# A two-layer decoder trunk on one core: operand offsets of the weight pieces, tried in the up projections

## The chip, the cores and the metric

The kernel runs on one core of a Trainium2 chip. The metric is the device time of one execution in microseconds (us); the time of a kernel is the median of its runs.

## The reference

The program computes two decoder layers on 256 tokens of width 2048, in float32, and a final RMSNorm. Each layer projects the normalised input once, runs three token mixers side by side (retention, dilated attention, a gated positional mixing), sends their 2048 channels through an output projection, and then a gated feed-forward with a short causal convolution. Cut to what matters here:

```python
proj = rms_norm(x, norm1_w) @ w_in                       # 2048 -> 6400
mixed = concat(retention(...), dilated_attention(...), chunk_gmlp(...))
x = x + mixed @ w_out                                    # 2048 -> 2048
h = rms_norm(x, norm2_w) @ w_up                          # 2048 -> 2 x 5632
gate, val = split(causal_conv3(h))                       # width 3, per channel
x = x + (silu(gate) * val) @ w_down                      # 5632 -> 2048
```

Nearly all the arithmetic is in the four weight matrices of each layer.

## The kernel before, in words

All weights lie in DRAM as one stream in the order in which they are used, 792 pieces of 128 x 1024 float32, 396 per layer. SyncE's queue loads a piece into a raw buffer (line 115). ScalarE writes a rounded copy of it, `hi` (line 140), and VectorE the rest, `lo` = raw - `hi` (line 150). The activations are split in the same way. A product is then three matmuls, hi x hi, hi x lo and lo x hi, so that a piece is always 24 matmuls of 128 x 128 by 256 columns. `Weights.take` (line 156) hands out the pieces and has them split three pieces ahead of their use; the order of all work is written out by hand, with generators that run small pieces of the mixers between the pieces of weights.

There are two kinds of stage. In the feature-major ones (`proj_t`, line 371, its matmul on line 388) a 128-column block of the piece is the stationary operand and the activations stream past it. These are the q and k projections (pieces 0 to 23 and 36 to 59 of a layer), the output projection (100 to 131) and the feed-forward (132 to 395). In the token-major ones (`proj_n`, line 417, matmul on line 428) the activations are stationary and the piece streams: pieces 24 to 35 (the v projection of the attention) and 60 to 99. `token_major` (line 81) tells which is which. The feed-forward has three parts of 96, 96 and 72 pieces; in each the first 64, 64 and 48 are the up projection and the others the down projection.

The mixers' own small float32 matmuls and transposes (lines 235 and 239, helpers) run between pieces: from piece 36 to the first pieces of the output projection, and for each norm. They set a flag, `stirred`.

`hi` and `lo` are tiles of 1024 + 64 columns in four buffers each, and the piece lies in its tile at an offset, in elements, that `place` (line 104) chooses when the split is issued:

```python
PLACES = ((32, 0), (0, 32))
...
    def place(self, p):
        other = self.stirred and p - self.moved >= APART
        if other:
            self.stirred, self.moved = False, p
        a = PLACES[token_major(p)][other]
        return slice(a, a + PIECE)
```

So a feature-major piece lies at 32 and a token-major one at 0; the first piece placed after small matmuls, at least four behind the last such, lies at the other of the two. It is called a moved piece below. In layer 0 these are 10, 14, 39, 43, 47, 51, 55, 59, 63, 75, 79, 83, 87, 91, 95, 99, 103, 107, 137 and 141; layer 1 has them at 401, 405 and then in the same places from 435 on, up to 537.

Of the kernel before, what the change touches and what calls it, by code (L numbers as in the profile page):

```python
# [27 lines left out]
P = 128  # L28
D = 2048
# [13 lines left out]
PIECE = 1024  # L43
# [7 lines left out]

SLACK = 64
PLACES = ((32, 0), (0, 32))
LAYER_PIECES = TOTAL // PIECE // DEPTH
QK_PIECES = 2 * H * D // PIECE
AV_PIECES = H * D // PIECE
REST_PIECES = (2 * H + 2 * G) * D // PIECE
APART = 4
FFN_PARTS = ((0, 16), (16, 32), (32, 44))


# [19 lines left out]
def token_major(p):  # L81

    p %= LAYER_PIECES
    a, b = QK_PIECES + AV_PIECES, 2 * QK_PIECES + AV_PIECES
    return QK_PIECES <= p < a or b <= p < b + REST_PIECES


class Weights:
# [13 lines left out]
        self.moved = 0  # L102

    def place(self, p):
        other = self.stirred and p - self.moved >= APART
        if other:
            self.stirred, self.moved = False, p
        a = PLACES[token_major(p)][other]
        return slice(a, a + PIECE)

    def load(self, upto):
# [69 lines left out]
def trunk_kernel(tc, x0, xt, stream, par, cst, wst, lnw, out):  # L181
# [5 lines left out]
    with ctx:  # L187
# [454 lines left out]
        for l in range(DEPTH):  # L642
# [124 lines left out]

            for i, (f0, f1) in enumerate(FFN_PARTS):
                last = i == len(FFN_PARTS) - 1
                QX[:] = [None] * NK  # L770
# [105 lines left out]
```

## Time and profile before

| | |
|---|---|
| median of 2 runs | 2243.12 us (2242.28 to 2243.97) |
| the profiled execution | 2242.37 us, span 2240.6 us |
| TensorE busy | 2223.4 us, 99% of the span |
| VectorE, ScalarE busy | 64%, 51% |
| granted TensorE clock, mean | 0.998 |
| DMA queue of the weights | 55.2% of 16 engines' span |

The busy time of TensorE adds up overlapping matmuls; how fast they follow each other is read from the length of a stretch over the number of matmuls in it. The chain of work that ended last lists such stretches, in order of time, by line.

### The profile page before, as it was taken

How to read it: one execution, taken by the hardware profiler on the slowest of the kernel's cores; microseconds unless marked ns; L12 is line 12 of the kernel's file. 1: busy time of each engine (PE TensorE's matmuls, PEld its weight loads, DVE VectorE, ACT ScalarE, POOL GpSimd, SP SyncE). 2: the span in 40 equal slices, each digit the busy share in tenths (PEclk: the TensorE clock that was granted, in tenths of full speed). 3: DMA queues.
4: the chain of work that ended last, by engine and by line, in shares of the span. 5: the costliest groups of instructions: out<-in, count | busy, mean ns of one | idle time of the engine just before them, and what ended most of it. 6: DMA issues, size and time to landing. Idle time of an engine off the chain costs nothing.

```text
span 2240.6 us, 45994 instructions
## 1 busy us (share of the span) xinstructions
PE 2223.4 (99%) x19430; PEld 2220.2 (99%) x19430; DVE 1443.3 (64%) x2086; ACT 1143.9 (51%) x1616; POOL 24.4 (1%) x38
## 2 busy tenths in 40 slices
PE   8999999999999999999999999999999999999997
PEld 8999999999999999999999999999999999999997
DVE  6466556677657775577754655666775577756775
ACT  6465455555435554455544745555554355434554
POOL 0000100000000000000000001000000000000000
PEclk9999999999999999999999999999999999999999
DMA  8545456565555555565565454555555565555553
GB/s 293 189 152 195 158 173 199 189 195 194 193 198 190 196 188 199 183 205 190 196 203 174 169 179 170 179 191 196 191 195 196 183 205 192 195 194 193 197 190 123
DMA packets 117135, 425.15 MB, mean 190 GB/s; under 512 B 12992, under 2 KB 12992, under 8 KB 116800
## 3 DMA queue, kind: packets, MB, share of 16 engines
q1 hardware_dynamic: 116928, 422.21, 55.2%
q8 instruction: 152, 2.49, 0.5%
q14 instruction: 55, 0.45, 0.1%
HBM read 420.06 MB, written 2.10 MB: 188 GB/s over the span
## 4 chain that ended last, share of the span: by engine, by line
PE 99%; DMA 0%; DVE 0%; SPq 0%; ACT 0%; POOLq 0%; issue 0%; DVEq 0%
PE mm L388 84%; PE mm L428 13%; PE mx L235 2%; PE mx L239 0%; DMA xg<-in_xt_dram 0%; DVE xg L786 0%; SPq L125 0%; SPq L261 0%; POOLq L870 0%; DVEq L870 0%; ACT p L290 0%; DVE diag L350 0%; DVE xg L718 0%; ACT t L312 0%; DVE ms L346 0%
## 5 line engine op out<-in xcount | busy, mean ns | idle before, releaser
L150 DVE TENSOR_TENSOR lo<-raw,hi 128x1024 fp32r<-128x1024 f32 (+1 forms) x793 | 969.3, 1223 | 694.1 <-ACT hi L140 693.6
L140 ACT ACTIVATE hi<-raw 128x1024 fp32r<-128x1024 f32 (+1 forms) x793 | 837.4, 1058 | 851.3 <-PE mm L388 459.5
L388 PE MATMUL mm<-p,hi 128*128 128x256 f32 x7168 | 1234.9, 277 | 5.7 <-ACT hi L140 5.1
L388 PEld LDWEIGHTS mm<-p,hi 128*128 128x128 f32 x7168 | 1085.1, 188 | 6.9 <-ACT hi L140 5.1
L388 PE MATMUL mm<-p,lo 128*128 128x256 f32 x3584 | 991.6, 277 | 0.0
L388 PEld LDWEIGHTS mm<-p,lo 128*128 128x128 f32 x3584 | 674.4, 188 | 0.5 <-DVE lo L150 0.2
L388 PE MATMUL mm<-q,hi 128*128 128x256 f32 x3840 | 655.2, 276 | 0.0
L388 PEld LDWEIGHTS mm<-q,hi 128*128 128x128 f32 x3840 | 578.6, 188 | 0.0
L388 PE MATMUL mm<-q,lo 128*128 128x256 f32 x1920 | 530.1, 276 | 0.0
L388 PEld LDWEIGHTS mm<-q,lo 128*128 128x128 f32 x1920 | 360.5, 188 | 0.0
L428 PE MATMUL mm<-hi,p 128*128 128x256 f32 x1664 | 273.8, 280 | 0.0
L428 PEld LDWEIGHTS mm<-hi,p 128*128 128x128 f32 x1664 | 232.3, 189 | 0.0
L428 PE MATMUL mm<-lo,p 128*128 128x256 f32 x832 | 180.2, 279 | 0.0
L750 ACT ACTIVATE a<-hs,prm 128x256 f32<-128x256 f32 x176 | 104.3, 593 | 63.3 <-DVE hs L402 63.3
L428 PEld LDWEIGHTS mm<-lo,p 128*128 128x128 f32 x832 | 133.8, 188 | 0.0
L753 DVE SCALAR_TENSOR_TENSOR a<-hs,prm,a 128x256 f32<-128x256 f32 x176 | 85.4, 485 | 6.3
L752 DVE SCALAR_TENSOR_TENSOR a<-hs,prm,a 128x256 f32<-128x256 f32 x176 | 84.2, 478 | 4.4 <-ACT a L750 4.4
L718 DVE TENSOR_TENSOR xg<-xg,mm 128x256 f32<-128x256 f32 x128 | 53.4, 419 | 39.3 <-PE mm L388 39.3
L402 DVE TENSOR_TENSOR hs<-mm,rbc 128x256 f32<-128x256 f32 x176 | 73.6, 418 | 2.7 <-PE mm L388 2.7
L756 ACT ACTIVATE a<-a 128x256 f32<-128x256 f32 x88 | 35.7, 405 | 33.5 <-DVE a L753 33.5
L312 ACT ACTIVATE t<-xg 128x256 f32<-128x256 f32 x75 | 30.1, 408 | 42.2 <-DVE xg L718 41.3
L762 ACT ACTIVATE q<-a 128x256 fp32r<-128x256 f32 x88 | 35.5, 404 | 3.5 <-DVE a L759 3.5
(107 smaller groups left out, 562.0 us busy)
## 6 DMA issues: line engine op xcount, KB each, us to landing
raw<-in_stream_dram SPq DMA_DIRECT2D x791, 512.0 KB, 3.8
out_dram<-xg SPq DMA_DIRECT2D x8, 256.0 KB, 2.4
xg<-in_xt_dram SPq DMA_DIRECT2D x3, 512.0 KB, 8.7
cs<-in_cst_dram SPq DMA_DIRECT2D x1, 1216.0 KB, 8.5
raw<-in_stream_dram SPq DMA_DIRECT2D x2, 256.0 KB, 4.1
ws<-in_wst_dram SPq DMA_DIRECT2D x2, 256.0 KB, 5.2
lw<-in_lnw_dram SPq DMA_DIRECT2D x2, 256.0 KB, 5.4
prm<-in_par_dram SPq DMA_DIRECT2D x1, 412.0 KB, 6.1
```

The lines of the kernel that those rows point to most:

```text
L140: self.nc.scalar.activation(hi[:, h], src[:, h], AF.Copy)
L150: self.nc.vector.tensor_tensor(lo[:, h], src[:, h], hi[:, h].bitcast(F32), op=ALU.subtract)
L235: T.matmul(*args, **kw)
L388: T.matmul(acc[m], w, v, start=k == 0 and i == 0, stop=k == n - 1 and i == 2)
L402: V.tensor_tensor(out, acc, norm["bc"], op=ALU.mult)
L428: T.matmul(acc[j][:, c], v, w[:, c], start=k == 0 and i == 0 and c.start == 0, stop=k == NK - 1 and i == 2, skip_group_check=True)
L718: V.tensor_tensor(X[m], X[m], acc, op=ALU.add)
L750: A.activation(a, hs[:, 2 : S + 2], AF.Identity, scale=conv_col(ch, 2), bias=conv_col(ch, 3))
L752: V.scalar_tensor_tensor(a, hs[:, 1 : S + 1], conv_col(ch, 1), a, op0=ALU.mult, op1=ALU.add)
L753: V.scalar_tensor_tensor(a, hs[:, 0:S], conv_col(ch, 0), a, op0=ALU.mult, op1=ALU.add)
L756: A.activation(a, a, AF.Silu)
L762: A.activation(q[:, 0:S], a, AF.Copy)
```

## The change

Two things change in `place`, and nothing else in the program. First, in the up projections the pieces go in groups of eight, and every other group lies at an offset from a list, 11 groups in each layer; between them the pieces lie as before. The list has 22 entries with 18 different values. Second, no token-major piece is moved any more, and the piece ahead of a token-major stage (23 and 59 of a layer) always is. By the flag's course through the program, the moved pieces of layer 0 are then 10, 14, 23, 39, 43, 47, 51, 55, 59, 100, 104, 108, 137 (141 falls into a tried group), and of layer 1 401, 405, 419, 435 and so on in the same places.

```diff
+TRIED = ((31, 33, 28, 36, 30, 34, 24, 40, 8, 56, 16), (48, 12, 20, 44, 52, 60, 4, 28, 33, 36, 56))
...
+FFN_AT = 2 * QK_PIECES + AV_PIECES + REST_PIECES + D * D // P // PIECE
...
     def place(self, p):
-        other = self.stirred and p - self.moved >= APART
+        last = token_major(p + 1)
+        other = not token_major(p) and (last or self.stirred and p - self.moved >= APART)
         if other:
             self.stirred, self.moved = False, p
         a = PLACES[token_major(p)][other]
+        q = p % LAYER_PIECES - FFN_AT
+        if q >= 0:
+            part, r = divmod(q, 96)
+            if r < (64, 64, 48)[part] and r // 8 % 2:
+                a = TRIED[p // LAYER_PIECES][part * 4 + r // 16]
         return slice(a, a + PIECE)
```

The tried groups of layer 0 are pieces 140 to 147, 156 to 163, 172 to 179, 188 to 195, then from 236 and from 332 on in the same rhythm, the last being 364 to 371; in layer 1 they are 396 later.

## Rows read from the trace of the kernel before

**Rows 1.** The page: busy time of the engines (share, instructions), granted clock in 40 slices.

```profile
PE 2223.4 (99%) x19430; PEld 2220.2 (99%) x19430; DVE 1443.3 (64%) x2086; ACT 1143.9 (51%) x1616; POOL 24.4 (1%) x38
...
PEclk9999999999999999999999999999999999999999
```

**Rows 2.** Waits of TensorE's matmuls: who for whom, us, times, longest.

```profile
PE mm L388 <- ACT hi L140: 5.1, 1, 5.1
```

**Rows 3.** The chain in order of time: start, length (us), engine, line, matmuls.

```profile
36.58 40.82 PE mm L388 x360
77.40 33.92 PE mm L428 x288
...
180.32 8.18 PE mm L388 x72
188.50 33.08 PE mm L428 x288
...
408.87 715.38 PE mm L388 x6312
...
1185.55 33.92 PE mm L428 x288
...
1517.02 709.96 PE mm L388 x6264
```

**Rows 4.** Timeline of TensorE around piece 63: start, length, line, operation, operands, count.

```profile
198.00 0.63 PE L428 MATMUL mm<-hi,p 128*128 128x256 f32 x4
...
198.71 0.63 PE L428 MATMUL mm<-hi,p 128*128 128x256 f32 x4
...
200.11 0.62 PE L428 MATMUL mm<-hi,p 128*128 128x256 f32 x4
...
200.79 0.62 PE L428 MATMUL mm<-hi,p 128*128 128x256 f32 x4
```

**Rows 5.** The same around piece 75, which runs from 233.78 to 236.61.

```profile
232.88 0.62 PE L428 MATMUL mm<-hi,p 128*128 128x256 f32 x4
...
233.56 0.62 PE L428 MATMUL mm<-hi,p 128*128 128x256 f32 x4
...
234.25 0.63 PE L428 MATMUL mm<-hi,p 128*128 128x256 f32 x4
...
234.96 0.63 PE L428 MATMUL mm<-hi,p 128*128 128x256 f32 x4
...
237.07 0.62 PE L428 MATMUL mm<-hi,p 128*128 128x256 f32 x4
...
237.75 0.50 PE L428 MATMUL mm<-hi,p 128*128 128x256 f32 x3
```

**Rows 6.** The chain from 218 to 330 us: token-major stretches between small matmuls.

```profile
231.21 13.73 PE mm L428 x120
...
246.90 5.56 PE mm L428 x48
...
253.80 14.14 PE mm L428 x120
...
268.60 8.29 PE mm L428 x72
...
281.50 14.14 PE mm L428 x120
```

**Rows 7.** The chain from 170 to 200 us: six transposes between two pieces.

```profile
179.67 0.65 PE mx L239 x6
```

**Rows 8.** The page's groups: the splits, and two VectorE operations of the convolution.

```profile
L150 DVE TENSOR_TENSOR lo<-raw,hi 128x1024 fp32r<-128x1024 f32 (+1 forms) x793 | 969.3, 1223 | 694.1 <-ACT hi L140 693.6
L140 ACT ACTIVATE hi<-raw 128x1024 fp32r<-128x1024 f32 (+1 forms) x793 | 837.4, 1058 | 851.3 <-PE mm L388 459.5
...
L753 DVE SCALAR_TENSOR_TENSOR a<-hs,prm,a 128x256 f32<-128x256 f32 x176 | 85.4, 485 | 6.3
L752 DVE SCALAR_TENSOR_TENSOR a<-hs,prm,a 128x256 f32<-128x256 f32 x176 | 84.2, 478 | 4.4 <-ACT a L750 4.4
```

## The prediction

> **What bounds the kernel now.** I read the page first, then the waits, then the chain, then single stretches of the timeline. The page shows TensorE busy 99% of the span, its clock granted in full in every slice [rows 1], that is the 2.4 GHz level. The waits show that it waits for its operands in one place only, 5.1 us at the start [rows 2]. So the time is the sum of the matmuls, and the only question is the pace at which they follow each other. The chain gives it, as length divided by count. In the feed-forward of layer 0 it is 715.38 us / 6312 = 113.3 ns, in that of layer 1 709.96 / 6264 = 113.3 ns; in the first token-major stage it is 33.92 / 288 = 117.8 ns, in both layers [rows 3]. Same shapes, same clock, two paces: I call them short (113.3) and long (117.8). A piece is 24 matmuls, so a piece at the long pace costs 24 x 4.45 = 107 ns more.
>
> What switches between them? The stretch of 288 matmuls that starts at 188.50 takes 33.08 us [rows 3]: 4 pieces long and 8 short (96 x 117.8 + 192 x 113.3 = 33.07). Its timeline shows where: six matmuls take 0.71 us up to 198.71 and 0.68 us after 200.11 [rows 4]. The fourth piece (63) is a moved one; the pace is long before and in it, short behind it. Around piece 75 it goes the other way: 0.68 us for six before it, 0.71 in it, 0.68 once it is over [rows 5]. So the pace depends on where the operands lie, it holds once taken, and a moved piece can reset it. It does not always: the stretches of 120 at 253.80 and 281.50 hold a moved piece each (83 and 91) and run at 117.8 throughout [rows 6]. By the tiles' addresses in the program, the stationary operand's start minus the moving one's is 64 modulo 256 bytes in an ordinary piece and 192 in a moved one, in both kinds of stage.
>
> **Tried offsets.** An offset a gives 64 + 4(a - 32) bytes. 22 groups of 8 pieces get one, 18 different values in all: 176 pieces, 4224 matmuls, all in stretches that run at 113.3 now. No instruction, transfer or wait is added. The trace shows one distance beside the ordinary one, 192, and it gives both answers: the 15 pieces at 36.58 hold two moved ones (10 and 14) and keep 113.4, each feed-forward stretch holds two (137, 141; 533, 537) and keeps 113.3 [rows 3], but piece 75 loses the short pace at once [rows 5]. For the 18 values I bound the cost from above by the long pace, the only other one in long stretches: 4224 x 4.45 = +18.8 us; and from below by the quickest pace of any matmul that loads as many weight columns, the transposes at 0.65 / 6 = 108.3 ns [rows 7]: 4224 x -5.0 = -21 us. The nearest rows are the two paces themselves, and they divide evenly, so I take half of the pieces at the long one: 88 x 0.107 = **+9.4 us**.
>
> Here a rule speaks for no effect at all. The Trainium skill, "TensorE: Matmul & The Clock Gate", Step-by-step: what each phase is for, has two independent read ports of the memory for the two operands, so that loading the next weights takes nothing from the running matmul. By that rule the tried offsets would cost 0; the trace disagrees so far, since the pace changes at piece 75, where the offset is all that changes.
>
> **Coming back.** Each group ends with a step back to the ordinary distance, 22 steps. Without small matmuls between, a moved piece at the long pace was followed by the short pace in three places that rows show (63, 75, 87 [rows 3, 5, 6], 87 by 8.29 us for 72, one long piece), against 83 and 91 where it stayed long; at 75 and 87 the pace before was short, at 83 and 91 long. So a return from a group entered at the short pace mostly restores it. I take two of some eleven long groups to stay long through the 8 pieces behind: 16 x 0.107 = **+1.7 us**; ends 0 and the whole feed-forward (below).
>
> **Token-major stages.** They are 52 pieces per layer. Piece by piece 36 of them are long now, 16 short: 12 of 12 and 4 of 12 in the stretches at 77.40 and 188.50 [rows 3], and by length over count of those behind 1 of 5, 1 of 2, 5 of 5, 1 of 3 and 5 of 5 [rows 6]; of eight more, which small matmuls cut up (72, 73, 89, 95 to 99), 7. A moved piece now stands ahead of each stage (23 and 59; 59 was one already), and the eight within (63, 75, 79, ..., 99) go. Piece 59 tells what the first does: it ran at the short pace (8.18 us for 72 with 57 and 58), and the stage behind it began at the long one all the same (4 long pieces) [rows 3]. So I expect 24 to 35 to stay long, and 60 to 71 to run long throughout, now that 63 resets nothing: the 33.08 us become 33.92, +8 pieces per layer. Against that 75, 87 and 99 are no longer moved and may stay short. Later pieces follow the small matmuls between, whose outcome I leave as it is. Net some +6 pieces per layer: 12 x 0.107 = **+1.3 us**. Ends: all of both stages short, -72 pieces, -7.7 us; all long, +32 pieces, +3.4 us. Behind the stage the moved pieces are 100, 104 and 108 where they were 103 and 107: at most a few pieces either way, **+0.3 us**.
>
> **Splits into odd offsets.** ScalarE and VectorE write and read the pieces at the new offsets. VectorE's reads of a row one element off (line 752) take 478 ns, from its start (line 753) 485 [rows 8]: nothing. If it were not nothing, a split of 1.06 + 1.22 us stands three pieces (8.2 us) ahead, and the two engines are busy 51% and 64% of the span [rows 1]. Without that lead the pair's 2.28 us would still fit a piece's 2.72. I cost it at 0. TensorE's own reads from offsets 31, 33, 30 and 34, five groups, 40 pieces, no row shows. The Trainium skill, "SBUF — State Buffer", Door 1: The DMA port swizzle, speaks of 16-byte lines with a penalty for each access that crosses to a new one; such a start would touch one line more, and the page has no price for it. I leave these groups in the half above.
>
> **Sum.** 9.4 + 1.7 + 1.3 + 0.3 = +12.7 us on the profiled execution's 2242.4 us, whose span is 2240.6; it lies 0.7 us under the median of 2243.1. That gives 2255 to 2256; I write **2255**.
>
> **Rivals.**
> - *The distance doesn't matter once the short pace is held.* (It is also what the rule of the two ports would give.) For it: the moved pieces of the feature-major stages at 36.58 and in the feed-forward lost nothing [rows 3], and all tried pieces are of that kind. Against it: piece 75. Then only the token-major and later terms are left: 2243 + 1.6 = 2245. Chance 0.22.
> - *The long pace sticks.* The first tried group (piece 140) takes it, and the step back restores nothing, as at 83 and 91 [rows 6]; nothing else in the feed-forward resets it, since no small matmuls run there. Pieces 140 to 395 and 536 to 791 would be long: 512 x 0.107 = 55 us, 2298, **slower** than before. It decides from 420 long pieces on (2%, 45 us). Against it: the returns at 63, 75 and 87. The full case 0.05; in part, or some distance with a pace above 117.8 that no row shows, between 2268 and 2288, another 0.11.
> - *A tried distance is better than the ordinary one,* or the moved piece ahead sets a whole stage to the short pace. 113.3 is not the floor of the engine [rows 7]. If a quarter of the groups went to 108.3, 44 pieces x 24 x 5 ns = 5 us would come back; with the stages short 7.7 more: 2243 - 13 = 2230. Against it: 792 pieces show two paces and neither is under 113.3. Chance 0.10.
> - *The forecast,* a third to two thirds of the tried pieces long: +6 to +12 us for them, 2247 to 2264 with the other terms. Chance 0.52.
>
> **Numbers.** The range 2237 to 2278 takes in the forecast, the first rival, the near half of the third and the near part of the second; some 0.15 is outside. 2% of this kernel is 45 us, about what a measurement can tell from no change. Over that on the fast side only all groups at 108.3 with both stages short and more would come (21 + 7.7 = 29 us): 0.01. On the slow side the sticking case with a little for a worse pace: 0.06. Within: 0.93.
>
> **What would show it.** In the chain after, length over count of the two feed-forward stretches: 113.3 ns throughout means that distance doesn't matter, 113.3 + 4.45/3 = 114.8 that all tried pieces (a third of them) are long. Group by group, 192 matmuls in 21.8 us or in 22.6. The stage at 188.50 at 33.08 or 33.92 us tells whether 63 did the reset; the one at 77.40 at 32.6 us would show that the moved piece ahead works, which I don't expect. A pace over 118 or under 113 in any group would prove my bounds wrong; an ordinary group at the long pace, that returns don't restore.

## The result and the profile after

The changed kernel takes 2272.65 us (2 runs, 2272.57 and 2272.73) against 2243.12: ratio 1.0135, 95% interval 1.0119 to 1.0152. That is 29.5 us slower, under 2%, inside the range of 2237 to 2278, and more than twice the 12 us that were forecast. The profiled execution took 2272.57 us, its span is 2270.8, 30.2 longer than before.

The page after: span and instructions, then busy time of the engines.

```profile
span 2270.8 us, 45994 instructions
...
PE 2253.6 (99%) x19430; PEld 2250.8 (99%) x19430; DVE 1443.2 (64%) x2086; ACT 1144.0 (50%) x1616; POOL 24.7 (1%) x38
```

The waits after: the longest of TensorE's.

```profile
PE mm L397 <- ACT hi L149: 5.1, 1, 5.1
```

TensorE's busy time grew by 30.2 us, as much as the span; VectorE's and ScalarE's are the same to 0.1 us, at the same counts [rows 1]. So no split became dearer. TensorE's waits are as before, the longest 5.1 us at the start [rows 2]: the matmuls follow each other more slowly. The chain of the kernel after (start, length, line, matmuls; line 397 is 388 of before, 437 is 428) has the places:

```profile
77.87 33.92 PE mm L437 x288
...
188.97 33.92 PE mm L437 x288
...
409.55 731.30 PE mm L397 x6312
...
1202.44 33.92 PE mm L437 x288
...
1313.54 33.92 PE mm L437 x288
...
1534.13 723.58 PE mm L397 x6264
```

Against [rows 3] the two feed-forward stretches grew by 15.9 and 13.6 us, 29.5 together; the stage at 77.87 is unchanged, and the one at 188.97 lost the short pace of its last eight pieces, 0.84 us. The same view cut to single groups in the feed-forward of layer 0, and to two of layer 1 (a cut shows one matmul more than the group's 192):

```profile
422.94 23.06 PE mm L397 x193
...
445.89 21.89 PE mm L397 x193
...
467.66 22.84 PE mm L397 x193
...
490.38 22.73 PE mm L397 x193
...
823.28 23.15 PE mm L397 x193
...
1067.12 67.96 PE mm L397 x577
...
1547.52 22.89 PE mm L397 x193
...
1903.65 22.52 PE mm L397 x193
```

Length over count: the group at offset 31 runs at 119.5 ns, the ordinary one behind it at 113.4; the group at 33 at 118.3, and the ordinary one behind it stays at 117.8; the group at 40 at 119.9 (120.0 by the starts of its matmuls). Behind the layer's last tried group (offset 16) all 24 pieces that are left run at 117.8. The last two rows are the groups at 48 and 4 of layer 1, at 118.6 and 116.7, the latter, with the group at 8, the quickest of all. The starts of the matmuls in the trace give each group's mean pace:

| distance, modulo 256 (offset) | ns a matmul | distance (offset) | ns a matmul |
|---|---|---|---|
| 64 (32), ordinary | 113.3 or 117.8 | 112 (44) | 120.0 |
| 192 (0), moved | 113.3 or 117.8 | 128 (48) | 118.6 |
| 0 (16) | 120.0 | 144 (52) | 119.9 |
| 16 (20) | 118.3 | 160 (56), twice | 120.0, 120.0 |
| 32 (24) | 118.3 | 176 (60) | 118.1 |
| 48 (28), twice | 118.3, 117.8 | 208 (4) | 116.7 |
| 56 (30) | 117.8 | 224 (8) | 116.7 |
| 60 (31) | 119.5 | 240 (12) | 117.3 |
| 68 (33), twice | 118.3, 118.3 | 80 (36), twice | 118.8, 118.8 |
| 72 (34) | 118.3 | 96 (40) | 120.0 |

No tried distance runs at the short pace. The table holds for these groups as they were entered here; in other kernels below, 208 and 240 run at another pace. Piece by piece against the trace of before the 30.2 us are: tried groups 22.4; pieces behind them that stay long 7.5 (69 pieces: 8 each behind 33, 28, 20, 60 and again 33, and behind 16 the 24 left and 5 of the next layer's first); token-major stages 0.6; output projection -0.2; the opening, pieces 0 to 23, 0.5; the end of the program -0.5 (rounded).

### The profile page after: what moved, and what is told of

The parts are those of the page before. It is cut to its first block, busy times and chain, and to the rows that moved or that the text cites. A ratio compares the mean times of both kernels' runs of the same rounds, so it can differ in the third digit from the quotient of the medians.

```text
span 2270.8 us, 45994 instructions
## 1 busy us (share of the span) xinstructions
PE 2253.6 (99%) x19430; PEld 2250.8 (99%) x19430; DVE 1443.2 (64%) x2086; ACT 1144.0 (50%) x1616; POOL 24.7 (1%) x38
## 4 chain that ended last, share of the span: by engine, by line
PE 99%; DMA 0%; DVE 0%; SPq 0%; ACT 0%; POOLq 0%; issue 0%; DVEq 0%
PE mm L397 84%; PE mm L437 13%; PE mx L244 2%; PE mx L248 0%; DMA xg<-in_xt_dram 0%; DVE xg L795 0%; SPq L134 0%; SPq L270 0%; POOLq L879 0%; DVEq L879 0%; ACT p L299 0%; DVE diag L359 0%; DVE xg L727 0%; ACT t L321 0%; DVE ms L355 0%
## 5 line engine op out<-in xcount | busy, mean ns | idle before, releaser
L397 PE MATMUL mm<-p,hi 128*128 128x256 f32 x7168 | 1262.6, 280 | 5.7 <-ACT hi L149 5.1
L397 PEld LDWEIGHTS mm<-p,hi 128*128 128x128 f32 x7168 | 1096.1, 189 | 6.8 <-ACT hi L149 5.1
L321 ACT ACTIVATE t<-xg 128x256 f32<-128x256 f32 x75 | 30.2, 409 | 41.5 <-DVE xg L727 40.6
```

The lines of the kernel that those rows point to most:

```text
L397: T.matmul(acc[m], w, v, start=k == 0 and i == 0, stop=k == n - 1 and i == 2)
```

## The experiments

The theory after the result: a matmul stream can hold 113.3 ns only where the stationary operand's start minus the moving one's is 64 or 192 bytes modulo 256; any other distance tried costs 3 to 7 ns a matmul; and at 64 or 192 the stream may still be stuck at 117.8, depending on how it was entered. Its rivals: the weights' own alignment counts, not the distance; the jump counts, not the distance; the new stage rule has a part in it. All kernels of this section but the two with a ratio were run once. The kernel before alone ranges from 2241.59 to 2244.65 us over its runs here, so totals 1 or 2 us apart say nothing by themselves; the readings rest on the lengths of stretches, such as the 715.38 us of the first feed-forward, which come back to the last digit wherever no piece changes its pace.

**The stage rule alone.** The changed kernel without the list.

```diff
-            if r < (64, 64, 48)[part] and r // 8 % 2:
+            if False and r < (64, 64, 48)[part] and r // 8 % 2:
```

> The rule for the token-major stages alone (a moved piece ahead of each, none within), no tried offsets. By the ledger of the changed kernel the two stages together gained 0.6 us and the output projection lost 0.2, so this should take 2243 to 2244 us, with the token-major pieces at the same paces as in the changed kernel: 24 to 35 and 60 to 71 long (117.8 ns a matmul), 95 to 99 short (113.3). If part of the 22 us of the tried groups came from the changed stages ahead of them, the feed-forward would show pieces at the long pace here too; I expect none.

Measured 2241.87 us, beside 2241.64 for the kernel before on the same chip. The chain:

```profile
77.10 33.92 PE mm L437 x288
...
188.20 33.92 PE mm L437 x288
...
408.79 715.38 PE mm L397 x6312
```

Both stages are long throughout, as in the changed kernel, and the feed-forward is as in [rows 3]. The rule has no part in the 29.5 us of the feed-forward; the 0.2 us between the two totals can't be told from nothing.

**The tried offsets alone.** The changed kernel with `place`'s first lines of before.

```diff
-        last = token_major(p + 1)
-        other = not token_major(p) and (last or self.stirred and p - self.moved >= APART)
+        other = self.stirred and p - self.moved >= APART
```

> The tried offsets alone, with the stage rule of before. By the ledger of the changed kernel the tried groups cost 22.4 us, the ordinary pieces behind them 4.4 in the up projections and 2.0 in the down projections, and some 0.5 at the second layer's start, which the first layer's last group leaves long. That is 29.3 us: 2271 to 2272 us. If the two parts of the change influence each other, the feed-forward would show other returns than in the changed kernel; I expect the same six.

Measured 2271.89 us. The chain:

```profile
188.27 33.08 PE mm L436 x288
...
408.64 731.30 PE mm L396 x6312
...
1533.01 723.58 PE mm L396 x6264
```

The feed-forward is that of the changed kernel to the last digit, with the same six returns stuck. The two parts add up and don't touch each other.

**Both operands 64 bytes further.** The kernel before with a longer tile in front of everything.

```diff
-        warm = cp.tile([P, 2], F32, name="warm")
+        warm = cp.tile([P, 18], F32, name="warm")[:, 16:18]
```

> The kernel before, with 64 bytes put in front of all the tiles that matmuls read, so that weights and activations both move by 64 bytes and the distance between them stays (64 modulo 256, 192 in moved pieces). Theory: only the distance counts; then 2242 to 2244 us and 113.3 ns in the feed-forward. Rival: the weights have to start at a multiple of 128 bytes, whatever the activations do; then every piece is at a longer pace, 792 x 24 x some 5 ns = +95 us, 2335 to 2340.

Measured 2241.91 us, beside 2241.64. The chain:

```profile
77.35 33.92 PE mm L428 x288
...
188.45 33.08 PE mm L428 x288
...
408.82 715.38 PE mm L388 x6312
```

Lengths equal to [rows 3] to the last digit, with all weights off the multiples of 128 bytes. So at this shift it doesn't matter where the operands lie, only how far apart. Other shifts of both were not run.

**Another distance everywhere, without jumps.**

```diff
-PLACES = ((32, 0), (0, 32))
+PLACES = ((48, 16), (16, 48))
```

> The kernel before with all offsets 16 elements higher: feature-major pieces at 48, moved ones at 16, token-major ones at 16 and 48. The distance is then 128 or 0 modulo 256 in every piece, and there are no jumps in the feed-forward but the two moved pieces. Theory (the short pace exists only at 64 modulo 128): all of the feed-forward runs at 118.5 to 120 ns, and the kernel takes 19008 x about 5.3 ns = 100 us less what is long already (10 us), 2325 to 2340 us. Rival (it is the jump from one distance to another that throws the matmuls into the long pace, and any distance holds the short one when left alone): 113.3 ns in the feed-forward, 2240 to 2250 us.

Measured 2336.09 us, 94 more than before, with the same instructions. The chain:

```profile
79.79 34.55 PE mm L428 x288
...
194.20 34.53 PE mm L428 x288
...
422.04 749.07 PE mm L388 x6312
...
1577.40 743.39 PE mm L388 x6264
```

749.07 / 6312 = 118.7 ns, the pace of the group at 48 in the table, now held through 263 pieces without a tried jump; the token-major stages, at distance 0, run at 120.0, as the group at 16 does. The distance is enough by itself.

**The same jumps to distance 192.** The tried groups at 0 and 64, which both give 192, with the stage rule of before.

```diff
-TRIED = ((31, 33, 28, 36, 30, 34, 24, 40, 8, 56, 16), (48, 12, 20, 44, 52, 60, 4, 28, 33, 36, 56))
+TRIED = ((0, 64) * 6, (64, 0) * 6)
...
-        last = token_major(p + 1)
-        other = not token_major(p) and (last or self.stirred and p - self.moved >= APART)
+        other = self.stirred and p - self.moved >= APART
```

> The tried groups at offsets 0 and 64 in place of the 18 values, stage rule as before: as many jumps, but the distance is 192 modulo 256 in each group, 64 modulo 128. Theory: the short pace is kept in all 22 groups and behind them, 113.3 ns throughout the feed-forward, 2242 to 2244 us. Rival (the jump does it): the groups run at 117.8 or more, 176 pieces x 0.107 to 0.13 = +19 to +23 us, 2262 to 2266.

Measured 2241.08 us. The chain:

```profile
408.08 715.38 PE mm L396 x6312
...
1516.23 709.96 PE mm L396 x6264
```

44 jumps, and not one matmul slower. With the run above this separates the two: the distance costs, the jump between 64 and 192 does not, in a feature-major stage that is at the short pace.

**Back by way of 192.** The changed kernel, the first piece behind each tried group at 0.

```diff
+            elif r and r % 16 == 0 and r <= (64, 64, 48)[part]:
+                a = 0
```

> The changed kernel, but the first piece behind each of the 22 tried groups lies at offset 0 (distance 192) and the next seven at 32 again. In the changed kernel 6 of the 22 returns stayed at 117.8 ns, 62 pieces, 6.6 us. Theory (the pace is a state that a jump of 128 bytes can reset where both distances are 64 modulo 128): in those six only the piece at 0 is long, 6 x 0.107 us, and some 6 us come back: 2266 to 2268 us. Rival (the reset works in token-major stages alone, as at piece 63, or the piece at 0 spoils returns that were short): as many long pieces behind the groups as before or more, 2272 us and up.

Measured 2269.8 us, 2.8 less than the changed kernel; neither theory's number. The chain:

```profile
409.89 727.03 PE mm L399 x6312
...
1529.89 724.60 PE mm L399 x6264
```

Layer 0 gained 4.3 us against the changed kernel, layer 1 lost 1.0. All six returns that were stuck came free. But three others, behind 48, 12 and 52 in layer 1, ran at 117.8 now, where they had run at 113.3 to 113.5, and of the 22 pieces at 192 themselves 11 were long. The group at 12 (distance 240), now entered from the long pace, also ran slower, at 119.9 ns, where it was entered from the short one in the changed kernel and ran at 117.3. The chain cut to this group, in the changed kernel:

```profile
1592.18 22.52 PE mm L397 x192
```

and here:

```profile
1588.80 23.03 PE mm L399 x192
```

A piece at 192 is no reset as such; it turns some returns one way and some the other.

**Token-major pieces at 192.**

```diff
-PLACES = ((32, 0), (0, 32))
+PLACES = ((32, 0), (32, 0))
```

> The kernel before, with the token-major pieces at 32 instead of 0, so that all of them have the distance 192 instead of 64; both are 64 modulo 128. Single moved token-major pieces have this distance in the kernel before and are long in all 16 places. Theory as it stands (64 modulo 128 admits the short pace): some stretches of these stages run at 113.3 as before, about 36 of 52 pieces long per layer, 2240 to 2245 us. Rival (in a token-major stage the short pace exists at 64 modulo 256 alone): all 104 pieces long, 32 more than now, +3.4 us, 2245 to 2246.

Measured 2241.5 us. The chain:

```profile
77.26 32.64 PE mm L428 x288
...
187.08 33.60 PE mm L428 x288
...
230.31 14.14 PE mm L428 x120
```

The first stage runs at 32.64 / 288 = 113.3 ns, all of it, which no run before it had shown. So 192 admits the short pace in a token-major stage too, against the rival; that the single moved pieces of the kernel before are long there in all 16 places must then come from how they are entered, which this run doesn't show by itself. Of the second stage only 60 to 62 are short; then comes moved piece 63, and behind it most pieces are long. The sum is near that of before: 33 long pieces per layer in these stages, elsewhere.

**No moved pieces.**

```diff
-PLACES = ((32, 0), (0, 32))
+PLACES = ((32, 32), (0, 0))
```

> The kernel before without any moved piece: feature-major pieces at 32, token-major ones at 0, always. It tells what the moved pieces are worth. If the feed-forward needs one behind the norm's small matmuls (137, 141) to be short, it runs at 117.8 from piece 134 on: +28 us per layer, 2298. I expect that it doesn't, since 135 is short before any is moved: then the token-major stages have as many long pieces as under the new rule (some 39 per layer), the feature-major ones perhaps fewer, since a moved piece behind small matmuls is mostly long itself, and the kernel takes 2240 to 2246 us.

Measured 2242.01 us, beside a median of 2242.16 for the kernel before. The chain:

```profile
77.44 33.92 PE mm L428 x288
...
188.37 33.92 PE mm L428 x288
...
408.97 715.38 PE mm L388 x6312
```

The moved pieces of the kernel before gained nothing in sum: what 63 frees is spent on moved pieces that are long themselves. Per layer the token-major stages have 39 long pieces where they had 36, and the feature-major pieces outside the feed-forward have fewer by as much (40, 55 and 103). The feed-forward needs none.

**Three moved token-major pieces per layer.**

```diff
-        other = self.stirred and p - self.moved >= APART
+        if token_major(p):
+            other = p % LAYER_PIECES in (25, 61, 79)
+        else:
+            other = self.stirred and p - self.moved >= APART
```

> The kernel before, with three token-major pieces moved per layer: 25, 61 (the second of each stage) and 79. Theory (a stage begins long by the change of roles, and a moved piece of distance 192 inside it resets that, as 63 does before): 26 to 35 and 62 to 71 run at 113.3, 80 too, and 95 to 99 as in the kernel with the new stage rule. 18 long pieces per layer in these stages instead of 36, and one less behind them: 38 x 0.107 = 4.1 us less, ratio 0.998. Rival (63 did it by where it stood, not by being moved): 24 to 35 stay long, ratio 1.000.

Measured 2238.38 us (11 runs) against 2242.16 (15 runs): ratio 0.9983, interval 0.9974 to 0.9992. The chain:

```profile
77.35 32.86 PE mm L431 x288
...
187.48 32.86 PE mm L431 x288
```

32.86 us is two long pieces and ten short ones (2 x 2.827 + 10 x 2.72), in both stages and both layers: the reset inside the stage works as at 63.

**Offsets by stretch.** Token-major pieces at 32 while the stage is entered and until the small matmuls begin, then at 0; nothing else moved but 79 and 81, and 91 at an offset from the list.

```diff
-        other = self.stirred and p - self.moved >= APART
-        if other:
-            self.stirred, self.moved = False, p
-        a = PLACES[token_major(p)][other]
+        q = p % LAYER_PIECES
+        a = 32
+        if q >= 73 and token_major(p) and q not in (79, 81):
+            a = (60, 28)[p // LAYER_PIECES] if q == 91 else 0
```

> Offsets chosen stretch by stretch from the paces seen so far: feature-major pieces never moved; token-major pieces 24 to 72, 79 and 81 at 32 (distance 192), the others at 0 (64); only piece 91 has another one, 60 in layer 0 and 28 in layer 1, to see whether that lets 92 to 94 out of the long pace. Theory (the pace of a stretch is set by the jump of distance at its beginning: a stage entered with the weights at 32 stays short, and a jump from 192 to 64 in the second piece behind twelve small matmuls ends the long pace): 24 to 35, 60 to 71, 73, 80 and 82 to 85 short, nine long pieces per layer in these stages instead of 36, and two less in the feature-major ones and one behind: 60 pieces or 6.4 us less, 2235.7 us, ratio 0.997. Rival (the three moved pieces that gave 0.9983 took what can be had): 82 to 85 and 73 stay long, ratio 0.998.

Measured 2236.75 us (10 runs) against 2242.49 (14 runs): ratio 0.9976, interval 0.9967 to 0.9986, the quickest kernel of the study. The chain:

```profile
77.25 32.64 PE mm L428 x288
...
186.91 32.64 PE mm L428 x288
...
251.65 14.14 PE mm L428 x120
...
279.24 13.86 PE mm L428 x120
```

Both stages begin with 12 short pieces. 81 to 85 (14.14 us for 120) stayed long, as did 73, against the expectation; in turn 91, at a distance of 80 or 208, ran long itself, and 92 to 94 behind it short, in both layers, where a piece at 192 had not helped [rows 6]. So the theory held for the entry of the stages and failed for 73 and 82 to 85, and the gain lies between the two that were named, 0.997 and 0.998, which the interval can't tell apart; that 73 and 82 to 85 stayed long is read from the trace.

## Why the prediction was wrong

**What bounds the kernel** held (beside the 5.1 us TensorE waits three more times, 3.1 us together, in both traces): TensorE alone, two paces at 64 and 192, a change that adds no instruction or wait. The splits into odd offsets cost nothing; the page after shows it (VectorE 1443.2 us, ScalarE 1144.0).

**Tried offsets** is the step that failed: "The nearest rows are the two paces themselves, and they divide evenly, so I take half of the pieces at the long one". All 176 pieces ran slower than 113.3, at 116.7 to 120.0 ns, 118.6 in the mean, so the term was 22.4 us and not 9.4; even the upper bound of 18.8 was under it, since the long pace of 117.8 was not the longest. The evidence lay in the trace and was read too narrowly. Both distances that it showed, 64 and 192, are 64 modulo 128, and the evenness of "kept at 192, lost at 192" said something of how a pace is entered, not of other distances. The constant offset of 16 more, and the jumps to 192, showed which it is.

**Coming back** failed in size: 69 pieces stuck, not 16, so 7.5 us and not 1.7. That returns "mostly" restore was right, 16 of 22; left out was how far a stuck one runs: behind offset 16 it lasted through the rest of the layer and into the next. The condition that it gave for a return, the short pace ahead of the group, did not sort them: of the 17 groups entered at the short pace 12 gave it back, and of the 5 entered at the long one 4 did.

**Token-major stages** held: 24 to 35 long, 60 to 71 long throughout, 33.92 us; the net was 0.6 us where 1.3 were forecast: 95 to 97 turned out short as well, 80 long.

The **rivals**: the first, that the distance doesn't matter once the short pace is held, fell with the first tried group. The second came true in part: the long pace stuck behind six groups, not everywhere, and paces above 117.8 exist; the 2268 to 2288 that it named for this case, with a chance of 0.11, hold the result. So the range held through this rival, not through the forecast. The third fell: no distance beat 113.3.

The rule of the Trainium skill, "TensorE: Matmul & The Clock Gate", Step-by-step: what each phase is for, that loading the next weights takes nothing from the running matmul, would let the distance between the operands cost nothing. The trace disagrees: the same 19008 matmuls and weight loads take 94 us more when one operand is 64 bytes further on, and the same time when both are. Whether it is the loading or the streaming that loses, no run shows. The 16-byte lines of the Trainium skill, "SBUF — State Buffer", Door 1: The DMA port swizzle, don't sort these paces: offsets 28 and 40, multiples of 16 bytes, run at 118.3 and 120.0, offsets 33 and 34, which are none, at 118.3.

What stays open: why 64 and 192 are the distances that admit the short pace, and what decides, behind small matmuls or behind another distance, which of the two paces a stream takes. Where two kernels share a stretch and what leads up to it, its paces are the same in both traces, the opening pieces apart. No run here shows the mechanism.

## What to carry to other kernels

When TensorE is busy all the time, divide the length of each stretch by its matmuls: two paces of the same matmul are a finding, and an average hides it. Where weights and activations are streamed in float32 tiles, choose the distance between the two operands' starts as deliberately as their size; here 64 modulo 128 bytes against 0 was worth 4%, at no instruction. And when a trace shows a quantity at two settings, ask what the two have in common before dividing the chances of a third evenly.

## What was not expected of the hardware

- The pace has sharp places: 4 bytes off the distance of 64 (60 and 68) already cost 6.2 and 5.0 ns of 113.3; of the 20 distances seen, two reach 113.3. Of the others 208 and 224 cost least in the changed kernel (116.7).
- In the up and down projections of every trace here the pace changed only at a change of the distance, or within four matmuls behind it. A stuck pace can last: 24 pieces, 576 matmuls, ran at 117.8 at the very distance that gives 113.3, outlasted the small matmuls of the next layer's norm, and came to an end behind a moved piece (401).
- Two groups at the same distance, 48, ran at 118.3 and 117.8, in the changed kernel and again with the tried offsets alone: the first entered from the long pace, the second from the short one. With the first entered from the short pace (back by way of 192) it ran at 117.8 too. At distance 240 the pace that it was entered from made more: 117.3 from the short one, 119.9 from the long one. And 208, at 116.7 in the feed-forward, ran at 118.5 in the token-major piece 91 (offsets by stretch). So a distance other than 64 and 192 has no one pace either.
